# Input projections of a hybrid encoder layer: from f32r pairs to stored, scaled f16 pairs

## The chip, the cores and the metric

The kernel runs on one core of one Trainium2 chip. The metric is the device time of one execution in microseconds (us), taken as the median of several runs. The engines are TensorE (PE in the profile; its weight loads are PEld), VectorE (DVE), ScalarE (ACT), GpSimd (POOL) and SyncE (SP), which here issues all DMAs; SPq is its queue.

## What is computed

One layer of a streaming encoder for 2048 tokens of width 1024. The parts that matter here:

```python
h = rms_norm(x, norm1_g)                  # x * rsqrt(mean(x^2) + eps) * g, by row
p = h @ w_in                              # 1024 x 2560, one combined projection
q, k, v = p[:, :512], p[:, 512:1024], p[:, 1024:1536]
gb, gc, hin, u = four groups of 256 columns
q, k = rms_norm per head of 64            # then banded attention, own chunk + 8 before
y_conv = gb * dwconv3_causal(gc * hin)
y_pool = trailing means of u, minus u, mapped by pool_w, scaled
x = x + concat(y_attn, y_conv, y_pool) @ w_out
x = x + square(relu(rms_norm(x) @ w1)) @ w2
```

## The kernel before

Tokens are worked off in four blocks of 512 (`block(b)`, line 333); activations of x stand transposed, 8 tiles of 128 channels by 512 tokens. A product that needs more than one 16-bit pass is written as three matmuls (`mm3`, line 158): high*high, high*low, low*high. In the projections, the high and low halves are f32r tiles: `load_w` (line 136) loads 128x512 weights, copies them to f32r (ACT, or POOL for `w_cp`, line 140) and subtracts (DVE, line 141), anew in every block. `load_x` (line 338) multiplies x by the gain and splits it in the same way, with no division by the row's norm; that factor (rstd) goes later into q and k (through eps), into v, and into conv and pool through the broadcast row `R`.

Each block has two stages. **Projections**: `project(0)`, `project(1)`, `project(2)` for q, k and v, 96 matmuls of 128x512 each (tiles `a`); meanwhile q and k are normalised per head (`normalize`, line 373) and the first heads prepared (`prep`, line 391: transposes `tk` and `tq`, a trip of k through DRAM, copies into `qs`, `qx`, `kx`). **Attention and side work**: `weave` (line 74) fixes PE's order: two steps of `attention` for each head and tile of 128 queries (32 such units), and between them, at `RATE` steps of side work for each of attention's (`RATE0` in block 0), `side()`: the output projection of the block before (`o`, line 663), then the conv and pool projections (`cp`, `dense`, line 566) with what follows from them. `pace` (line 696) puts a step of the *survey* in at 2 of every 7 side steps: each loads two 256 KB tiles of w1 or w2 (`pr`, `ps`) and squares them on ACT, for the scales of the MLP. The survey's tiles, like those of x, take turns in a ring of three buffers, tag `x` of the pool `scr`.

A scheduler that simulates the program places everything that `weave` doesn't order: on ACT, DVE, POOL and in the DMA queue of SP it sets the order, and each engine works its list off in that order. After the four blocks comes the MLP (lines 721 to 955), whose matmuls are f16 (`b_u`, `b_d`) and which the change doesn't touch.

## Time and profile before

| | |
|---|---|
| runs | 2157.41, 2162.93, 2163.63 us, median 2162.93 |
| profiled execution | 2157.06 us, of which the span from first to last instruction is 2155.3 |
| PE busy | 2060.9 us, 96% of the span, 11136 matmuls |
| DVE busy | 1372.5 us, 64% |
| ACT busy | 1014.8 us, 47% |
| POOL busy | 700.5 us, 33% |
| mean granted TensorE clock | 0.983 of full speed |
| DMA | 378.19 MB, 55.3% of 16 engines' span |

Busy time is the union over an engine's instructions. Matmuls overlap in it: a single one is shown with some 0.4 us, yet the next starts after half of that, so their pace is read from starts. PEclk is the granted clock: 1.00 is 2.4 GHz, and half of it, 1.2 GHz, is the only other level; a mean between tells how much of a stretch ran at either.

### The profile page before, as it was taken

The numbers are of one execution on the slowest core, as the hardware profiler recorded it, in microseconds if no ns is written. First come the engines' busy times: TensorE is split into PE (matmuls) and PEld (weight loads), VectorE is DVE, ScalarE is ACT, GpSimd is POOL, SyncE is SP. The second block draws the span as 40 slices with busy tenths as digits, with TensorE's granted clock in tenths as the row PEclk, the third lists the DMA queues.
The fourth block names the chain that finished last, engine by engine and source line by source line (L and its number), as shares of the span: only waits on it lengthen the run. The fifth ranks groups of instructions, "written<-read, shape, count | busy, mean of one in ns | idle before, by whom it ended". The sixth has DMA issues, their size and how long they took to land.

```text
span 2155.3 us, 31723 instructions
## 1 busy us (share of the span) xinstructions
PE 2060.9 (96%) x11136; PEld 1269.3 (59%) x11136; DVE 1372.5 (64%) x2177; ACT 1014.8 (47%) x1939; POOL 700.5 (33%) x565
## 2 busy tenths in 40 slices
PE   8999999999899999989999889999999999999999
PEld 6777787878787878744444334444444444444444
DVE  7677566856577557897757897767743044253354
ACT  6465465646565655545647346446234151150330
POOL 4233054502211022365535555445522031030132
PEclk9999999999899999989999999999999999999999
DMA  8674587548754786654444684447843333333344
GB/s 298 179 216 154 171 261 218 169 142 251 224 172 140 223 236 183 212 176 158 168 157 147 239 279 142 167 156 269 276 121 102 103 103 100 101 97 108 103 143 155
DMA packets 207759, 378.19 MB, mean 175 GB/s; under 512 B 24688, under 2 KB 31984, under 8 KB 207600
## 3 DMA queue, kind: packets, MB, share of 16 engines
q1 hardware_dynamic: 207600, 376.18, 55.3%
q8 instruction: 87, 1.43, 0.3%
q14 instruction: 72, 0.59, 0.1%
HBM read 261.26 MB, written 98.04 MB: 167 GB/s over the span
## 4 chain that ended last, share of the span: by engine, by line
PE 71%; DVE 9%; DMA 7%; issue 5%; POOL 4%; ACT 3%; SPq 1%; POOLq 0%; DVEq 0%; ACTq 0%
PE b_d L787 20%; PE b_u L787 17%; PE a L159 4%; PE a L161 4%; PE a L160 4%; PE cp L159 2%; PE pt L497 2%; PE cp L160 2%; PE cp L161 2%; PE o L159 2%; PE o L161 2%; PE o L160 2%; PE y L512 2%; PE s L476 1%; PE s L477 1%
## 5 line engine op out<-in xcount | busy, mean ns | idle before, releaser
L787 PE MATMUL b_d<-ft_u,s_d 128*128 128x512 f16 x1152 | 264.6, 379 | 6.0 <-DVE ft_u L738 3.6
L787 PEld LDWEIGHTS <-s_u 128*128 128x128 f16 x1536 | 150.4, 98 | 197.2 <-issue 16.5
L787 PEld LDWEIGHTS <-s_d 128*128 128x128 f16 x1536 | 150.2, 98 | 190.6 <-issue 9.9
L908 DVE TENSOR_TENSOR acc<-acc,b_d 128x512 f32<-128x512 f32 x176 | 119.2, 682 | 184.4 <-PE b_d L787 181.3
L787 PEld LDWEIGHTS <-a_d 128*128 128x128 f16 x1152 | 113.3, 98 | 147.1 <-issue 13.0
L787 PEld LDWEIGHTS <-a_u 128*128 128x128 f16 x1152 | 112.6, 98 | 144.1 <-issue 9.5
L771 POOL TENSOR_TENSOR t1u<-u2u,c11u 128x512 f32<-128x512 f32 x32 | 42.5, 1329 | 439.2 <-ACT u2u L894 427.0
L787 PE MATMUL b_d<-fb_u,a_d 128*128 128x512 f16 x768 | 183.4, 379 | 0.0
L159 PE MATMUL a<-wq,xg 128*128 128x512 f32 x384 | 152.4, 402 | 8.2 <-ACT wq L140 8.0
L161 PE MATMUL a<-wq,xg 128*128 128x512 f32 x384 | 154.2, 402 | 2.1 <-DVE xg L344 2.1
L160 PE MATMUL a<-wq,xg 128*128 128x512 f32 x384 | 153.3, 399 | 0.0
L486 ACT ACTIVATE sb<-sb,nm 128x640 f32<-128x640 f32 (+4 forms) x128 | 97.7, 763 | 108.8 <-DVE nm L480 107.2
L499 DVE SCALAR_TENSOR_TENSOR pp<-pt,pp 128x384 f16<-128x384 f32 (+1 forms) x224 | 102.5, 483 | 66.8 <-ACT pp L498 65.8
L787 PE MATMUL b_u<-xt,s_u 128*128 128x512 f16 x576 | 132.5, 384 | 11.4 <-ACT xt L737 6.0
L208 POOL TENSOR_TENSOR acc<-acc,sq 128x512 f32<-128x512 f32 x56 | 83.0, 1482 | 184.8 <-ACT sq L207 143.4
L787 PE MATMUL b_u<-zt,s_u 128*128 128x512 f16 x576 | 126.9, 379 | 0.0
L480 DVE CUSTOM_DVE_ANT_0 sb<-s,b 128x640 f32<-128x640 f32 (+4 forms) x128 | 93.9, 734 | 36.3 <-PE s L477 34.9
L159 PE MATMUL o<-mix,wo 128*128 128x512 f32 x256 | 108.6, 425 | 2.7 <-DVE xo L678 2.7
L140 POOL CAST wc<-rwc 128x512 fp32r<-128x512 f32 x64 | 41.2, 643 | 211.1 <-PE cp L161 92.2
L159 PE MATMUL cp<-xg,wc 128*128 128x512 f32 x256 | 109.5, 428 | 0.0
L141 DVE TENSOR_TENSOR wq<-rwq,wq 128x512 fp32r<-128x512 f32 x96 | 77.5, 815 | 48.8 <-ACT wq L140 48.7
L285 POOL TENSOR_TENSOR pq<-pq,pq 128x512 bf16<-128x512 bf16 x32 | 38.3, 1196 | 208.4 <-ACT pq L282 207.7
(267 smaller groups left out, 4696.1 us busy)
## 6 DMA issues: line engine op xcount, KB each, us to landing
rwq<-w_qkv SPq DMA_DIRECT2D x96, 256.0 KB, 2.9
pr<-w SPq DMA_DIRECT2D x64, 256.0 KB, 4.0
rwc<-w_cp SPq DMA_DIRECT2D x64, 256.0 KB, 4.1
rwo<-w_out SPq DMA_DIRECT2D x64, 256.0 KB, 3.7
ps<-w SPq DMA_DIRECT2D x64, 256.0 KB, 4.0
r_u<-w SPq DMA_DIRECT2D x64, 256.0 KB, 2.9
wd<-s_u SPq DMA_DIRECT2D x64, 256.0 KB, 2.4
r_d<-w SPq DMA_DIRECT2D x64, 256.0 KB, 2.9
```

What stands on the lines that cost most here:

```text
L141: (lo or ve).tensor_tensor(out=w[:, 1], in0=raw, in1=w[:, 0].bitcast(F32), op=ALU.subtract)
L159: te.matmul(out, ah, bh, start=start, stop=False)
L160: te.matmul(out, ah, bl, start=False, stop=False)
L161: te.matmul(out, al, bh, start=False, stop=stop)
L208: gp.tensor_tensor(out=acc, in0=acc, in1=q, op=ALU.add)
L480: ve.tensor_tensor_reduce(out=sb[:, :nk].rearrange("p (e k) -> p e k", e=ne), in0=s[:, :ne, :hk], in1=bi[:, 640 - nk :].rearrange("p (e k) ...
L486: exps.append(sc.activation(sb[:, :nk], sb[:, :nk], AF.Exp, bias=nmx, scale=-1.0, accum_out=st["l"][:, i, j : j + 1]))
L497: te.transpose(pt[:, m * P : (m + 1) * P], sb[:, c0 + m * P : c0 + (m + 1) * P], ident)
L499: ve.scalar_tensor_tensor(out=pp[:, 1, c0:c1], in0=pt[:, :n], scalar=PSC, in1=pp[:, 0, c0:c1], op0=ALU.mult, op1=ALU.subtract)
L512: te.matmul(st["y"][:, i, j], pp[:, pi, ms_], vv[:, vi], start=(m == 0 and r == 0), stop=(m == nkt - 1 and r == 2))
L787: te.matmul(bank, w[:, a, q * P : (q + 1) * P], xs[q][:, c], start=start and q == 0 and i == 0, stop=q == n - 1 and i == 2, skip_group_che ...
L908: ve.tensor_tensor(out=a, in0=a, in1=bk, op=ALU.add)
```

## The change

Every input projection gets f16 halves. `weight_scale` finds a power of two for each of four weight groups (q, k, v, conv+pool) from the largest absolute weight: `look` takes a maximum of each 128x512 tile on DVE, a transposing matmul (`mx`) and a reduction bring them together. In block 0 `make_pair` scales and splits the weights (ACT and DVE), two tiles to a pair, and writes each pair to DRAM (`wq16`, `wc16`); the later blocks load pairs of 512 KB with `load_pair`, without ACT, DVE or POOL. `next_x` now normalises rows before the split: it sums squares, makes rstd, broadcasts it into `rn`, and then scales each tile by gain and `rn` on DVE, copies it to f16 on ACT and subtracts on DVE. For blocks 1 to 3 it runs as part of the side work of the block before, with x loaded twice (`xs`, `x`) through the `x` ring; for block 0 it runs at the start, from tiles that stay. `R` and the factors by it go. The survey leaves block 0 and takes every third side step in blocks 1 to 3. `RATE0` is 0.5.

```diff
-RATE, RATE0 = 0.95, 0.45
+RATE, RATE0 = 0.95, 0.5
...
+    def load_pair(src, name, shape):
+        w = wsp.tile([P, 2, 2, 512], F16, tag="w", name=name)
+        sy.dma_start(w.rearrange("p k s n -> p (k s n)"), src.rearrange("p k n -> p (k n)"))
...
+    def make_pair(raws, dst, scale, name, shape):
+        w = wsp.tile([P, 2, 2, 512], F16, tag="w", name=name)
+        for k in range(2):
+            raw = raws[k]()
+            sc.activation(w[:, k, 0], raw, AF.Copy, scale=scale)
+            ve.scalar_tensor_tensor(out=w[:, k, 1], in0=raw, scalar=scale, in1=w[:, k, 0], op0=ALU.mult, op1=ALU.subtract)
+        sy.dma_start(dst.rearrange("p k n -> p (k n)"), w.rearrange("p k s n -> p (k s n)"))
...
+    def largest(m, nm):
+        t = pd("mx" + nm)
+        te.matmul(t[:, :P], m.broadcast_to([P, P]), ident, start=True, stop=True)
+        ve.tensor_reduce(out=m, in_=t[:, :P], axis=AX.X, op=ALU.max)
...
+    def look(raw, i):
+        ve.tensor_reduce(out=wm[:, i : i + 1], in_=raw, axis=AX.X, op=ALU.max, apply_absolute_value=True)
+
+    def weight_scale(c):
+        m = const.tile([P, 1], F32, name=f"mw{c}")
+        ve.tensor_reduce(out=m, in_=wm[:, 8 * c : 8 * c + (8 if c < 3 else 16)], axis=AX.X, op=ALU.max)
+        r, inv = largest(m, str(c))
+        ve.tensor_scalar(wscale[:, c : c + 1], inv, 8192.0, None, op0=ALU.mult)
...
+    def look_at_cp(i):
+        raw = scr.tile([P, 512], F32, tag="x", bufs=3, name=f"sc{i}")
+        sy.dma_start(raw, w_cp[i // 2, i % 2])
+        look(raw, 24 + i)
...
+        acc = po.tile([P, TB], F32, tag="acc2", name=f"accn{b}")
+        for k in range(KT):
+            sumsq(acc, part(k, "xs"), k == 0, scr)
+            yield
+        ms = token_cols(acc, f"ms1_{b}")
+        yield
+        r = rsqrt(sm, ms, NT, "r1")
+        rb = row_bcast(r, f"rb{b}")
+        rn = p1.tile([P, TB], F32, tag="rn", bufs=1, name=f"rn{b}")
+        sc.copy(rn, rb)
+        yield
+        for k in range(KT):
+            xr = part(k, "x")
+            ve.scalar_tensor_tensor(out=xr, in0=xr, scalar=g1s[:, k : k + 1], in1=rn, op0=ALU.mult, op1=ALU.mult)
+            sc.copy(xgs[k][:, 0], xr)
+            ve.tensor_tensor(out=xgs[k][:, 1], in0=xr, in1=xgs[k][:, 0], op=ALU.subtract)
+            yield
...
             for k in range(KT):
-                if c == 0:
-                    load_x(k)
-                w = load_w(w_qkv[c, k], f"wq{b}_{c}_{k}", 1)
...
+                if k % 2 == 0:
+                    if b:
+                        pair = load_pair(wq16[c, k // 2], f"wq{b}_{c}_{k}", 1)
+                    else:
+                        raws = [lambda j=j: first_raws[c % 2][:, j] for j in (k, k + 1)]
+                        pair = make_pair(raws, wq16[c, k // 2], wscale[:, c : c + 1], f"wq{b}_{c}_{k}", 1)
+                if b == 0:
+                    if c < 2:
+                        fetch(c + 1, k)
+                    if c:
+                        look_at_cp(8 * c - 8 + k)
...
-                    ve.tensor_tensor(out=hs, in0=t, in1=R, op=ALU.mult)
+                    sc.activation(hs, t, AF.Copy, scale=sback)
...
-                if 2 * n % 7 < 2:
+                if b and n % 3 == 0:
                     next(surveyed, None)
...
+            ahead = next_x(b + 1, nxgs) if nxgs else iter(())
+            for _ in c:
+                next(ahead, None)
+                yield
```

Where the instructions stand, at three places.

DVE at the start of block 0, before: x and weights are split tile by tile, from the 14th instruction on (`bi` and `nb` belong to the attention's bias tables).

```order
L184 TENSOR_TENSOR pw<-pwr,pw 128x256
L344 SCALAR_TENSOR_TENSOR xg_0_123<-x_0_136,col,xg_0_123 128x512
L141 TENSOR_TENSOR wq_0_0_143<-rwq_0_0_141,wq_0_0_143 128x512
L344 SCALAR_TENSOR_TENSOR xg_1_124<-x_1_158,col,xg_1_124 128x512
L141 TENSOR_TENSOR wq_0_1_167<-rwq_0_1_165,wq_0_1_167 128x512
```

The same with the change: this stretch stands behind 16 looks at the weights of q and k (`first`); `r1r` is the last step of rstd, `sc` a look at a tile of w_cp.

```order
L285 TENSOR_SCALAR wscale<-big_208 128x1
L289 RECIPROCAL epsc<-back 128x1
L279 TENSOR_REDUCE wm<-sc_501 128x1
L188 TENSOR_TENSOR r1r<-r1r,r1t 128x4
L290 TENSOR_TENSOR epsc<-epsc 128x1
L279 TENSOR_REDUCE wm<-sc_521 128x1
L156 SCALAR_TENSOR_TENSOR wq_0_0_270<-first,wscale,wq_0_0_270 128x512
```

So rstd's end and the first weight pair now come after all these looks; the 8 scalings of x follow after the 8 subtractions for q's weights.

DVE in block 0 between the projections of k and of v, before: four weight tiles of v (`wq_2`) are split ahead of k's normalisation (`ssk`, later `nk`).

```order
L141 TENSOR_TENSOR wq_2_0_637<-rwq_2_0_635,wq_2_0_637 128x512
L141 TENSOR_TENSOR wq_2_1_685<-rwq_2_1_683,wq_2_1_685 128x512
L141 TENSOR_TENSOR wq_2_2_702<-rwq_2_2_700,wq_2_2_702 128x512
L141 TENSOR_TENSOR wq_2_3_719<-rwq_2_3_717,wq_2_3_719 128x512
L378 TENSOR_REDUCE ssk_652<-sqk_0_653 128x8
```

With the change, where `a_1` are the sums of k's projection and `mx_661` is the matmul that gathers v's largest weight; on PE it stands behind the last matmul of k's projection.

```order
L491 TENSOR_TENSOR nk_786<-a_1_2_490,rqr 128x512
L491 TENSOR_TENSOR nk_786<-a_1_3_491,rqr 128x512
L266 TENSOR_REDUCE mw_659<-mx_661 128x1
L267 TENSOR_SCALAR mw_659<-mw_659 128x1
L246 TENSOR_SCALAR big_665<-mw_659 128x1
L247 TENSOR_TENSOR pow_666<-big_665,mw_659 128x1
L248 TENSOR_TENSOR pow_666<-pow_666,big_665 128x1
L249 TENSOR_TENSOR pow_666<-pow_666,mw_659 128x1
L250 RECIPROCAL big_665<-pow_666 128x1
L286 TENSOR_SCALAR back<-pow_666,gm 128x1
L309 TENSOR_REDUCE vm<-vn 128x1
L285 TENSOR_SCALAR wscale<-big_665 128x1
```

v's scale, and with it every weight pair of v, now comes after all of k's normalisation.

ACT in block 1, in the second half of attention, before: exponentials (`sb`), copies of transposed scores (`pp`) and the survey (`pq`).

```order
L486 ACTIVATE sb_5_0_4218,l_2_3911<-sb_5_0_4218,nm_5_0_4219 128x640
L282 ACTIVATE pq_0_4249<-pr_0_4247 128x512
L282 ACTIVATE pq_1_4253<-pr_1_4251 128x512
L498 ACTIVATE pp_4_3_4258<-pt_4_3_0_4259 128x384
L498 ACTIVATE pp_4_3_4258<-pt_4_3_384_4265 128x256
L486 ACTIVATE sb_5_1_4312,l_2_3911<-sb_5_1_4312,nm_5_1_4313 128x640
```

The same two exponentials with the change, where `xs` are tiles of the next block's x.

```order
L591 ACTIVATE sb_5_0_4142,l_2_3861<-sb_5_0_4142,nm_5_0_4143 128x640
L341 ACTIVATE pq_0_4173<-pr_0_4171 128x512
L341 ACTIVATE pq_1_4177<-pr_1_4175 128x512
L746 ACTIVATE uh<-cp_7_4008,back 128x512
L223 ACTIVATE sq<-xs_1_4247 128x512
L603 ACTIVATE pp_4_3_4182<-pt_4_3_0_4183 128x384
L603 ACTIVATE pp_4_3_4182<-pt_4_3_384_4189 128x256
L223 ACTIVATE sq<-xs_2_4285 128x512
```

Between two exponentials stand two more squares of freshly loaded tiles and a copy of conv and pool's sums.

## Rows read from the trace of the kernel before

**Rows 1.** Windows by stage: length, busy time (count) by engine, PEclk, DMA share, GB/s.
```profile
8.00:82.00 74.00, 74.00 (x317) 59.54 (x318) 58.55 (x120) 38.83 (x67) 24.84 (x22) 1.00 0.78 252
82.00:172.00 90.00, 81.51 (x587) 67.99 (x586) 69.23 (x167) 54.96 (x135) 33.99 (x40) 0.94 0.71 210
172.00:243.00 71.00, 69.85 (x329) 56.00 (x328) 46.87 (x83) 33.13 (x58) 14.58 (x12) 1.00 0.46 144
252.00:410.00 158.00, 153.05 (x1217) 131.84 (x1217) 109.81 (x223) 97.03 (x210) 70.15 (x82) 0.97 0.71 221
...
486.00:646.00 160.00, 154.56 (x1204) 133.11 (x1203) 110.24 (x224) 98.38 (x237) 34.46 (x38) 0.96 0.72 215
...
721.00:882.00 161.00, 153.31 (x1211) 132.19 (x1210) 106.93 (x222) 98.20 (x241) 27.61 (x29) 0.97 0.67 198
```

**Rows 2.** Waits of PE up to 1000 us: total us, times, longest.
```profile
PE a L161 <- DVE xg L344: 2.1, 3, 1.2
```

**Rows 3.** Timeline of PE, block 0's projections: two starts, 45 matmuls apart.
```profile
48.02 0.40 PE L160 MATMUL a<-wq,xg 128*128 128x512 f32 x1
...
58.56 0.40 PE L160 MATMUL a<-wq,xg 128*128 128x512 f32 x1
```

**Rows 4.** Chain that ended last, in the MLP: start, us, what.
```profile
1571.22 72.52 PE b_u L787 x336
```

**Rows 5.** Timeline of PE, first matmuls of the program: start, duration.
```profile
10.69 0.63 PE L160 MATMUL a<-wq,xg 128*128 128x512 f32 x1
11.11 0.63 PE L161 MATMUL a<-wq,xg 128*128 128x512 f32 x1
```

**Rows 6.** Windows, second 20 us: the columns of rows 1.
```profile
20.00:40.00 20.00, 20.00 (x91) 16.29 (x90) 17.56 (x42) 14.79 (x25) 9.45 (x8) 1.00 0.99 338
```

**Rows 7.** Tile x up to 45 us: ns min/median/max, first and last start.
```profile
L340 SPq DMA_DIRECT2D x<-xT x8: 327/328/432, 2.1 to 18.0; - x8
L343 ACT ACTIVATE xg<-x,col x8: 717/724/728, 6.0 to 23.2; 128x512 fp32r<-128x512 f32 x8
L344 DVE SCALAR_TENSOR_TENSOR xg<-x,col,xg x8: 736/1130/1801, 6.7 to 24.6; 128x512 fp32r<-128x512 f32 x8
...
DMA to landing us min/median/max: 3.8/4.9/5.2
```

**Rows 8.** Groups of DVE, 42 to 82 us: busy us, mean ns, idle before.
```profile
L141 DVE TENSOR_TENSOR wq<-rwq,wq 128x512 fp32r<-128x512 f32 x11 | 7.4, 687 | 4.3 <-ACT wq L140 4.3
...
L378 DVE TENSOR_REDUCE ssk<-sqk 128x8 f32<-128x512 f32 x4 | 2.7, 683 | 0.0
```

**Rows 9.** Timeline of ACT, k's normalisation in block 0.
```profile
54.30 2.71 ACT L377 ACTIVATE sqk<-a 128x512 f32<-128x512 f32 x4
```

**Rows 10.** Timeline of DVE, from k's normalisation to v's scale in block 0.
```profile
57.83 0.69 DVE L141 TENSOR_TENSOR wq<-rwq,wq 128x512 fp32r<-128x512 f32 x1
...
59.88 0.69 DVE L141 TENSOR_TENSOR wq<-rwq,wq 128x512 fp32r<-128x512 f32 x1 [0.34 <-ACT wq L140]
...
61.15 2.48 DVE L383 TENSOR_TENSOR nk<-a,rqr 128x512 f32<-128x512 f32 x4
...
67.58 0.69 DVE L250 TENSOR_REDUCE vm<-vn 128x1 f32<-128x512 f32 x1 [1.38 <-PE vn L248]
...
69.78 0.15 DVE L254 TENSOR_SCALAR vsc<-big 128x1 f32<-128x1 f32 x1
```

**Rows 11.** Timeline of PE, end of block 1's projections.
```profile
241.01 0.60 PE L396 MATMUL tq<-ident,nq 128*128 128x128 f32 x4
...
245.42 1.05 PE L221 MATMUL rb<-ident,r1r 128*128 128x128 f32 x8
...
251.34 0.38 PE L476 MATMUL s<-kx,qs 128*128 128x320 f32 x1 [3.48 <-DMA qs<-qlo]
```

**Rows 12.** Chain in block 1's attention.
```profile
323.36 6.30 DMA kx<-kd
329.73 5.17 DMA pr<-w
```

More of the change, by code (lines that the diff above doesn't have):

```diff
@@ L224, in trunk @@
     vsc = const.tile([P, 2], F32, name="vsc")
[L225 removed]
+    vacc = p1.tile([P, 512], F32, tag="rn", bufs=1, name="vacc")
     def power_above(p):
@@ L365, in project, with fetch @@
             return ac
+        if b == 0:
+            kept = [p1.tile([P, NT, TB], F32, tag="n" + nm, name=f"x0{nm}") for nm in "qk"]
+            raw2 = po.tile([P, 2, KT, TB], F32R, tag="mix", name="first")
+            first_raws = [raw2[:, i].bitcast(F32) for i in range(2)]
+            def fetch(c, k):
+                raw = first_raws[c % 2][:, k]
+                sy.dma_start(raw, w_qkv[c, k])
+                look(raw, 8 * c + k)
+                if c == 2:
+                    value_norms(k, raw)
+                if k == KT - 1:
+                    weight_scale(c)
+            gain_scale()
+            steps = next_x(0, xgs, kept)
+            for k in range(KT):
+                next(steps)
+            for k in range(KT):
+                fetch(0, k)
+            for _ in steps:
+                pass
         acq = project(0)
-        ms1 = token_cols(acc, f"ms1_{b}")
-        rstd = rsqrt(sm, ms1, NT, "r1")
-        epsq = sm.tile([P, NT], F32, tag="epsq", name=f"epsq{b}")
-        ve.tensor_scalar(epsq, ms1, EPS, None, op0=ALU.mult)
         def normalize(ac, nm):
@@ L448, in block @@
         acv = project(2, lambda k: next(steps) if k in EARLY else None)
[L449 to L451 removed]
+        if b == 0:
+            weight_scale(3)
         for i in range(NT):
             src = acv[i].rearrange("p (h d) -> p h d", h=H)
[L454 to L455 removed]
+            sc.activation(v[:, :, i, 0], src, AF.Copy, scale=vback)
+            ve.scalar_tensor_tensor(out=v[:, :, i, 1], in0=src, scalar=vback, in1=v[:, :, i, 0], op0=ALU.mult, op1=ALU.subtract)
         if b < NB - 1:
@@ L458, in block @@
                 sy.dma_start(vd[b % 2, h], v[:, h].rearrange("p t s d -> p (t s d)"))
-        rb = row_bcast(rstd, f"rb{b}")
-        sc.copy(R, rb)
         mix = po.tile([P, 2, KT, TB], F32R, tag="mix", name=f"mix{b}")
@@ L567, in dense @@
             t = pd(f"cp{b}_{g}")
+            pair = weights.next()
             for half in range(2):
-                w = weights.next()
+                w = pair[:, half]
                 for kk in range(4):
@@ L643, in convpool @@
                     ve.tensor_copy(uh[:, j, 0:16], uh[:, j, TB : TB + 16])
-                ve.tensor_tensor(out=uh[:, j, 16:], in0=t, in1=R, op=ALU.mult)
+                sc.activation(uh[:, j, 16:], t, AF.Copy, scale=sback)
                 yield
@@ L702, in block, with raw_cp @@
         cp_order = (6, 7, 0, 1, 2, 3, 4, 5)
-        cp_loads = [lambda g=g, half=half: load_w(w_cp[g, half], f"wc{b}_{g}_{half}", 4, **CPW(gp, ve, g, half)) for g in cp_order for half in range(2)]
+        if b:
+            cp_loads = [lambda g=g: load_pair(wc16[g], f"wc{b}_{g}", 4) for g in cp_order]
+        else:
+            def raw_cp(g, half):
+                raw = wraw.tile([P, 512], F32, tag="raw", name=f"rwc{g}_{half}")
+                sy.dma_start(raw, w_cp[g, half])
+                return raw
+            cp_loads = [lambda g=g: make_pair([lambda h=h: raw_cp(g, h) for h in range(2)], wc16[g], wscale[:, 3:4], f"wc{b}_{g}", 4) for g in cp_order]
         prev_loads, prev_outproj, prev_stats = prev_out
@@ L712, in side @@
                 yield
-            yield from c
+            ahead = next_x(b + 1, nxgs) if nxgs else iter(())
+            for _ in c:
+                next(ahead, None)
+                yield
+            for _ in ahead:
+                yield
         weave(tc, attention(first), pace(side()), RATE if b else RATE0)
-        return out_loads, outproj, stats
-    prev_out = ([], lambda w: (), lambda: ())
+        return (out_loads, outproj, stats), nxgs
+    prev_out, xgs = ([], lambda w: (), lambda: ()), x_pairs(0)
     for b in range(NB):
-        prev_out = block(b, prev_out)
+        prev_out, xgs = block(b, prev_out, xgs)
     scales()
```

78 lines of the change are left out of this document (49 added, 29 removed).

## The prediction

> **What bounds the kernel now.** I read the stages first [rows 1]. Up to 882 us TensorE is busy nearly throughout: in the projections it is idle for 0 us of 74 in block 0 and 1.2 of 71 in block 1. DVE is busy for 59 of 74 us at the start and ACT for at most 62% anywhere, so before 882 us the time is TensorE's stream plus its gaps. The gaps lie in attention: 8.5 us in block 0, then 5.0, 5.4 and 7.7 us, 18.1 in blocks 1 to 3. After a gap the clock is at its lower level for a while; one minus the mean clock, times the stretch, is what that costs: 5.4 us in block 0, and 4.7, 6.4 and 4.8, 15.9 us, in the others. All that can be won by removing gaps is therefore 34 us in blocks 1 to 3 and 14 us in block 0's attention.
>
> Then the pace of one matmul. 45 f32r matmuls of the projections took 58.56 - 48.02 = 10.54 us, 234.2 ns each [rows 3]; 336 f16 matmuls of the same size in the MLP took 72.52 us, 215.8 ns each [rows 4]. The difference is 18.4 ns. All other work of the change must hide behind this stream or lengthen it.
>
> **Faster matmuls.** 1920 matmuls change type: 3 x 96 for q, k, v and 192 for conv and pool, in each of four blocks. Block 0's q, k and v I cost with its start, below. For the rest: 192 in block 0's attention save 3.5 us, 864 in the later projections 15.9 us and 576 in the later attentions 10.6 us: 30.0 us in all.
>
> The Trainium skill ("TensorE: Matmul & The Clock Gate", section "Wait — 56ns, not 53.3ns?") gives the start-to-start time at the full clock as the columns over 2.4 GHz plus 2.5 ns, 215.7 ns for 512 columns, and ties it to no type. By that, the f16 rows agree and the f32r rows do not; by the page alone this term would be nothing and the sum 30 us higher.
>
> **Block 0's start.** Today the first matmul starts 8 us into the span and projections end at 82 [rows 1]. With the change, nothing runs before x's row norms and q's weight scale, and both need complete passes. I follow the lists of the section on the change, in us from the start of the span.
> - *Loads.* 24 tiles (x, weights of q, of k) are issued ahead. The first lands at 2.1 + 3.8 = 5.9 [rows 7]; at the 338 GB/s seen with the DMAs 99% busy [rows 6] each further one takes 0.78 us. x is there at 11.3, q's weights at 17.5, k's at 23.7.
> - *Scale and norm.* A look costs 0.68 us [rows 8] and keeps up with the loads. The last step of rstd stands behind all 16 looks, two bias steps and one look at w_cp: about 28.
> - *Splits.* Then DVE does 8 subtractions for q's weights at 0.74 (the short form of L344 [rows 7]) with two more looks, until 35, 8 scalings of x until 41, two looks and bias steps, and 8 subtractions for x from 44 to 50. Matmuls of the high halves can start at 37, but the stream only flows from 44.6.
> - *q.* 90 matmuls are left. Some ten run at the lower clock, at 0.42 us [rows 5]; the rest at 215.8 ns. End: 66.
> - *k.* Its scale stands behind 8 looks at v's weights and 10 at w_cp. The latter share three buffers, each with some 4.9 us from issue to landing [rows 7]. I get 63 for the scale and 65 for the first pair if all DVE work takes its short form. L344's median was 1.13 us, against 0.74 at least [rows 7], and POOL sums squares beside this; for 8 subtractions that is 3 us. I take 68, hence k's end at 68 + 96 x 0.2158 = 88.7.
> - *v.* Its scale now waits for k's end and stands behind k's normalisation. Before, that work went from 54.30 to 63.63 [rows 9, 10], with two subtractions of 0.69 between that now are gone, and the steps from a maximum to a scale took 67.58 to 69.93, 2.4 us [rows 10]. The squares start some 2 us before k's projection ends, so v's scale is there at 88.7 - 2 + 8.0 + 2.4 = 97, and the ACT copy of 0.72 [rows 7] gives the first weights at 98; with handovers I say 99. TensorE stands still for 10 us here, restarts at the lower clock (2 us) and ends at 99 + 20.7 + 2 = 122.
>
> So block 0's projections end at 122 and not 82: **40 us lost**. Bounds: if scalings and subtractions overlap the looks better and the second gap of 7.6 us vanishes, 32; if all 40 scalings and subtractions take 0.39 us more, and half of that shows, and the loads land slower, 50. I take 40, the value that the short forms and one correction give.
>
> The Trainium skill ("SBUF — State Buffer", "SBUF: two separate sides") says that a DVE instruction with two SBUF inputs and a GpSimd instruction that reads SBUF exclude each other for a whole instruction. By that the 3 us above are what seven POOL sums cost; if the rule did not bite, k would start at 66 and the loss be 38. L344's spread is in favour of it.
>
> **Block 0's attention.** DVE loses 15 weight subtractions and 8 multiplications by `R`, and gains 8 subtractions for w_cp and 16 instructions of `next_x`, about as much; ACT loses the survey's squares and gains copies. No change beyond the 3.5 us, with 14 us of gaps as the bound of a gain.
>
> **Blocks 1 to 3.** The weights' copies and subtractions go: 120 subtractions at 0.69 us at least [rows 8], over 80 us of DVE. DVE has slack there, so this alone gives nothing. PE's waits for split x at a block's start, 2.1 us, go [rows 2]. The first scores of a block waited 3.5 us for a DMA that follows the transposes `tq` [rows 11]; what covers that DMA shrinks, by the `rb` matmuls (0.8 us, moved away) and 18 matmuls at 18.4 ns: 1.1 us a block, **3.4 us lost**. The pair loads move as many bytes as the f32 loads did, at DMA shares of 0.46 [rows 1]: hidden; if that cover went, the projections would wait for 512 KB every 5.2 us.
>
> Attention's gaps are the open price. The chain there runs through a transfer of `kx` (6.30 us), then the survey's `pr` (5.17 us), for which ACT waits with the next copies of scores queued behind it [rows 12]. The change does not shorten these transfers. It puts 22 survey steps in each block instead of 19, and in blocks 1 and 2 sends 16 more tiles of x through the same three buffers, whose ACT instructions stand between the exponentials. Bounds: all gaps vanish, -34 us; or buffers limit: in the second half of attention 22 survey tiles and 16 of x, each holding a buffer for 4.9 us of landing and about 2 of use, take 38 x 6.9 / 3 = 87 us, in a half of some 75: 12 us too long in each of two blocks, +25. I take +4, near the middle, since what ends these waits is not touched and the traffic rises by little.
>
> **Sum:** 40 - 30.0 - 2.1 + 3.4 + 4 = +15.3 us. The profiled execution took 2157.06 us, so 2172.4 on its scale; the median of the runs shown is 5.9 us higher, and I forecast 2178.2 against it. About 0.3%, 6.5 us, is what can be told from no change here.
>
> **Rivals.**
> - *Gaps close* (0.22). If DVE's and POOL's load, not the DMAs, sets the gaps, half of the 48 us goes: 40 - 30.0 - 2.1 + 3.4 - 24 = -12.7, 2150. It decides if ACT's waits in attention end with DVE. For it: 80 us less DVE work, and scores waiting on DVE in block 0; against it: the chain through DMAs [rows 12].
> - *A cheaper start* (0.20). 32 us instead of 40, gaps as they are: 32 - 30.0 - 2.1 + 3.4 = +3.3, 2166, no change that can be told.
> - *The ring of three* (0.17). ACT waits for x tiles in blocks 1 and 2: +25 in place of +4, 2199. For it: the two families of tiles alternate in one ring. Against it: mean DMA shares of 0.71 and 0.72 leave room [rows 1].
> - *One pace for both types* (0.02). If f16 matmuls with these operands start 234 ns apart, as the f32r ones do, the 30.0 us fall away: +45.3, 2208. Only the MLP's f16 matmuls were seen at 216 ns [rows 4], with other operands; that the type sets the pace is likelier by far. The Trainium skill's rule above would lead to this rival.
>
> **How the numbers follow.** My own forecast has 0.39. Faster by over 0.3%: 0.22; within 0.3%: 0.20; slower: 0.39 + 0.17 + 0.02 = 0.58. The range goes from 2147 to 2202: it leaves out the lower half of the first rival, half of the third and the last, about 2 in 10. The forecast's own range, from its start's bounds, is 2170 to 2188.
>
> **What would show it.** Matmuls of `a` and `cp` start 216 ns apart. The first of them starts near 37 us, flow begins near 45, and block 0's projections end near 122, with TensorE idle for some 10 us just before v's. In blocks 1 and 2, ACT's waits for `x`, `xs`, `pr` and `ps` add up to about what they were. I am wrong about the start if v's projection begins before 90 us, and about the gaps if TensorE's idle time in attention of blocks 1 to 3 falls under 10 us or rises above 30.

## The result and the profile after

The changed kernel takes **2226.28 us**, median of four runs (2218.37 to 2234.78), beside 2160.17 us for the kernel before (2154.24 to 2163.63): ratio **1.0314, 95% interval 1.0277 to 1.035**. It is slower by 66 us, not by 15, and lies outside the range. The profiled execution is the slowest of the four, 2234.78 us with a span of 2232.9, so the stages below hold 8.5 us more than the median does.

| us | before | after | forecast of the difference |
|---|---|---|---|
| span's start to block 0's first scores | 82.8 | 126.9 (+44.1) | +40 |
| attention of blocks 0, 1, 2 | 88.8, 157.3, 159.0 | 98.3, 182.1, 173.3 (**+48.6**) | -10.5 by pace, +4 by gaps |
| attention of block 3 | 157.4 | 154.4 (-3.0) | -3.5 |
| projections of blocks 1, 2, 3 | 79.7, 76.5, 75.7 | 70.4, 69.7, 72.3 (-19.5) | -14.6 |
| last projection work and the MLP | 1278.1 | 1285.4 (+7.3) | 0 |

A stage runs from one first start on TensorE to the next: attention from a block's first scores to the next block's first `a` (in block 3 to the first matmul `mx` of the MLP's scales), projections from there to the next first scores. The MLP's code is the same; from its first matmul to the end of the span it took 1254 to 1266 us in the profiles of this study, so its few us are scatter.

Windows of after by these stages (columns of [rows 1]; attention of block 0, projections of 1, and so on in turn):

```profile
126.92:225.20 98.28, 84.56 (x603) 54.07 (x604) 67.34 (x170) 55.06 (x133) 7.58 (x6) 0.91 0.66 201
225.20:295.58 70.38, 66.06 (x331) 31.72 (x331) 24.79 (x53) 17.83 (x31) 2.25 (x3) 0.99 0.41 121
295.58:477.60 182.02, 159.74 (x1195) 120.49 (x1196) 102.26 (x211) 107.80 (x228) 72.37 (x77) 0.91 0.74 223
...
547.33:720.70 173.37, 151.95 (x1196) 115.58 (x1197) 99.91 (x212) 107.81 (x243) 46.95 (x47) 0.95 0.75 228
...
793.01:947.40 154.39, 147.43 (x1163) 113.75 (x1164) 88.28 (x192) 101.17 (x253) 15.62 (x13) 0.96 0.72 217
```

The same stretches of before:

```profile
82.84:171.60 88.76, 80.27 (x582) 67.27 (x582) 68.03 (x163) 53.95 (x133) 33.59 (x40) 0.94 0.70 210
251.34:408.60 157.26, 152.48 (x1213) 131.80 (x1214) 108.41 (x222) 95.63 (x207) 68.83 (x81) 0.97 0.72 221
485.10:644.10 159.00, 153.47 (x1197) 132.43 (x1197) 108.34 (x221) 96.48 (x233) 34.46 (x38) 0.96 0.72 216
719.80:877.20 157.40, 149.66 (x1163) 129.18 (x1164) 102.70 (x213) 96.05 (x237) 27.61 (x29) 0.97 0.69 203
```

Length minus PE busy is TensorE's idle time: 8.5 + 4.8 + 5.5 + 7.7 = 26.5 us before, 13.7 + 22.3 + 21.4 + 7.0 = 64.4 after, 38 us more. One minus PEclk, times the length, is what the lower clock took: by these rounded values 21 us before, 40 after, 19 us more (16 if only the time in which matmuls ran is counted). Block 3, whose attention carries no `next_x`, lost nothing, though the survey is as dense there as in blocks 1 and 2: 37 of its loads are issued in that attention, 31 before.

Timeline of PE in after, block 0's start (start, duration, what, idle before and its releaser):

```profile
33.76 0.61 PE L175 MATMUL a<-wq,xp 128*128 128x512 f16 x1 [5.62 <-ACT xp L423]
...
41.38 0.61 PE L177 MATMUL a<-wq,xp 128*128 128x512 f16 x1 [4.88 <-DVE xp L424]
...
65.10 0.38 PE L176 MATMUL a<-wq,xp 128*128 128x512 f16 x1 [1.18 <-DVE wq L156]
...
94.20 0.76 PE L265 MATMUL mx<-ident,mw 128*128 128x128 f32 x2 [6.75 <-DVE nk L491]
...
99.03 1.44 PE L175 MATMUL a<-wq,xp 128*128 128x512 f16 x3 [1.17 <-ACT wq L155]
...
122.45 0.38 PE L177 MATMUL a<-wq,xp 128*128 128x512 f16 x1
122.67 0.38 PE L175 MATMUL cp<-xp,wc 128*128 128x512 f16 x1
122.88 0.38 PE L176 MATMUL cp<-xp,wc 128*128 128x512 f16 x1
```

This is the start as forecast: first matmul at 33.8 (37), flow from 41.4 (44.6), k's first pair at 65.1 (65 to 68), k's end at 94.20 - 6.75 = 87.4 (88.7), v's start at 99.0 (99), the end at 122.7 (122). The last three starts are 216 ns apart.

The long stops in the middle of attention, in blocks 1 and 2, stand before `ms`, the matmuls of the next block's row norms:

```profile
437.20 1.84 PE L229 MATMUL ms<-ones,accn 128*128 128x1 f32 x8 [5.68 <-DVE mix L719]
...
442.69 1.92 PE L237 MATMUL rb<-ident,r1r 128*128 128x128 f32 x8
...
683.31 1.84 PE L229 MATMUL ms<-ones,accn 128*128 128x1 f32 x8 [8.42 <-DVE mix L719]
```

The releaser is no producer of `accn`: `mix` reads `pl`, the earlier tenant of the PSUM bank that `ms` is written to. The chain of waits in after, 396 to 450 us, shows what made `mix` late:

```profile
413.17 3.21 DMA xs<-xT
416.46 0.63 ACT sq L223
...
423.66 6.50 DMA xs<-xT
430.25 0.63 ACT sq L223
430.88 0.64 ACT pp L603 x2
431.52 0.42 issue
431.94 0.73 ACT yc L733
432.69 1.23 DVE yc L734
433.94 1.52 DVE yc L735
435.46 0.94 DVE z L729
436.40 0.67 DVE mix L719
437.20 1.84 PE ms L229 x8
```

ACT stands at `sq` until the transfer of an x tile lands; behind it in ACT's queue stand the copies of transposed scores (`pp`) and `yc`; DVE's steps on `yc` wait for that, and `mix` stands behind them in DVE's queue. ACT's waits for DMAs in block 1's attention (295.58 to 477.60 us; total, times, longest), and the one kind of the same stage before:

```profile
ACT pq L341 <- DMA pr<-w: 17.8, 8, 7.0
ACT sq L223 <- DMA xs<-xT: 8.0, 6, 2.0
...
ACT accn L220 <- DMA xs<-xT: 4.2, 1, 4.2
```

```profile
ACT pq L282 <- DMA pr<-w: 5.4, 4, 3.9
```

In blocks 1 and 2 together ACT waited 15.2 us for `pr`, `ps` and `xs` before and 54.8 after; the forecast's sign was that these waits stay about what they were. In block 0, where no survey runs, it is DVE that stands, at the second load of x (`x`), and the copies of scores behind it stop TensorE; DVE, then PE, in after:

```profile
181.15 0.75 DVE L422 SCALAR_TENSOR_TENSOR x<-x,g1s,rn 128x512 f32<-128x512 f32 x1 [6.55 <-DMA x<-xT]
```

```profile
182.16 0.24 PE L617 MATMUL y<-v,pp 128*128 128x64 f16 x1 [4.68 <-DVE pp L604]
```

### The profile page after: what moved, and what is told of

Its sections match the earlier page's. It is cut to its first block, busy times and chain, and to the rows that moved or that the text cites. A ratio compares the mean times of both kernels' runs of the same rounds, so it can differ in the third digit from the quotient of the medians.

```text
span 2232.9 us, 31343 instructions
## 1 busy us (share of the span) xinstructions
PE 2054.8 (92%) x11146; PEld 1108.4 (50%) x11146; DVE 1303.6 (58%) x2146; ACT 997.5 (45%) x1905; POOL 648.9 (29%) x501
## 4 chain that ended last, share of the span: by engine, by line
PE 58%; DMA 14%; DVE 14%; issue 5%; ACT 4%; POOL 4%; SPq 1%; POOLq 0%; DVEq 0%; ACTq 0%
PE b_d L905 20%; PE b_u L905 17%; DMA xs<-xT 3%; PE a L175 2%; PE a L176 2%; PE a L177 2%; PE pt L602 2%; DMA r_d<-w 2%; PE o L175 1%; PE cp L175 1%; DMA pr<-w 1%; PE cp L176 1%; PE cp L177 1%; PE o L176 1%; PE o L177 1%
## 5 line engine op out<-in xcount | busy, mean ns | idle before, releaser
L1026 DVE TENSOR_TENSOR acc<-acc,b_d 128x512 f32<-128x512 f32 x176 | 119.3, 682 | 185.5 <-PE b_d L905 182.2
L175 PE MATMUL a<-wq,xp 128*128 128x512 f16 x384 | 147.8, 387 | 7.5 <-ACT xp L423 5.6
L177 PE MATMUL a<-wq,xp 128*128 128x512 f16 x384 | 146.9, 384 | 4.9 <-DVE xp L424 4.9
L176 PE MATMUL a<-wq,xp 128*128 128x512 f16 x384 | 148.1, 386 | 1.2 <-DVE wq L156 1.2
L905 PE MATMUL b_u<-zt,s_u 128*128 128x512 f16 x576 | 126.9, 379 | 0.0
L175 PE MATMUL o<-mix,wo 128*128 128x512 f32 x256 | 111.3, 436 | 6.4 <-DVE xo L780 5.8
L602 PE MATMUL pt<-ident,sb 128*128 128x128 f32 x560 | 86.7, 278 | 27.8 <-DVE pp L604 24.1
L176 PE MATMUL o<-mix,wo 128*128 128x512 f32 x256 | 105.6, 413 | 0.0
L177 PE MATMUL o<-mix,wo 128*128 128x512 f32 x256 | 105.5, 412 | 0.0
L175 PE MATMUL cp<-xp,wc 128*128 128x512 f16 x256 | 101.9, 398 | 2.9 <-ACT r2s L794 2.9
```

What stands on the lines that cost most here:

```text
L175: te.matmul(out, ah, bh, start=start, stop=False)
L176: te.matmul(out, ah, bl, start=False, stop=False)
L177: te.matmul(out, al, bh, start=False, stop=stop)
L602: te.transpose(pt[:, m * P : (m + 1) * P], sb[:, c0 + m * P : c0 + (m + 1) * P], ident)
L905: te.matmul(bank, w[:, a, q * P : (q + 1) * P], xs[q][:, c], start=start and q == 0 and i == 0, stop=q == n - 1 and i == 2, skip_group_che ...
L1026: ve.tensor_tensor(out=a, in0=a, in1=bk, op=ALU.add)
```

## The experiments

Three theories for attention at first. **Ring**: the second load of x through three buffers stops ACT, and ACT stops TensorE. **Bank**: `ms` and `rb` wait for a PSUM bank that the pool branch holds. **Survey pace**: the survey's steps are too dense beside `next_x`. Two more came up on the way: **load** (ACT and DVE have too much to do beside the exponentials) and **order** (two small matmul groups stand in TensorE's fixed order and stop it whenever their input is late). Each table gives the time from the span's start to the end of block 0's attention, since work moves across the first scores, then attention of blocks 1, 2, 3.

### x loaded once, and the bank

`e1_one_load` loads x once, three tiles ahead, into the place where its pair will lie; squares and scaling read it there, and no raw tile of x goes through the ring (the scaled tile still takes a buffer of it). `e2_psum_t` only moves `ms` and `rb` to another bank; `e3_one_psum` does both; `e4_no_survey` is after without the survey.

```diff
-            xr = part(k, "x")
+            return xgs[k].rearrange("p s n -> p (s n)").bitcast(F32)
...
+            load(k + 3)
+            sumsq(acc, place(k), k == 0, scr)
```

```diff
-        ms = token_cols(acc, f"ms1_{b}")
+        ms = token_cols(acc, f"ms1_{b}", "t")
-        rb = row_bcast(r, f"rb{b}")
+        rb = row_bcast(r, f"rb{b}", "t")
```

> Edit: the next block's x is loaded once, straight into the memory of the f16 pair that it will become, three tiles ahead; the squares and the scaling both read it there. The second load of each tile goes, and no load of x passes through the ring of three any more. Attention (first scores to the first matmul of the next projection, or to the matmuls of the last scale in block 3) took 98.3, 182.0, 173.4 and 154.4 us in blocks 0 to 3 of the changed kernel, 88.8, 157.4, 159.0 and 157.3 before. Theory 'ring': ScalarE waits for x tiles behind three shared buffers and holds the copies of scores back. Then attention of blocks 1 and 2 falls by 12 us or more each, and the whole by 30 or more. Rival 'bank': the matmuls of the row norms wait in TensorE's order for one of two PSUM banks that a dense group holds; then no more than 10 us go. Rival 'survey pace': no more than 10 us go.

> Edit: only the PSUM tiles ms1 and rb of the next block's row norms move from the tag d (two banks, of which an open dense group holds one) to the tag t (three banks). Theory 'ring': only the waits of ms themselves can go, 5.7 us in block 1 and 8.4 in block 2, so at most 14 us and likely under 8. Rival 'bank': attention of blocks 1 and 2 falls by 12 us or more each, and the whole by 25 or more. Rival 'survey pace': under 8 us.

> Both edits: x loaded once into the pair's memory, and ms1 and rb in the tag t. If either theory, ring or bank, names the whole cause between them, attention of blocks 0 to 2 comes to what block 3 shows, the stage before the change less 3 us (some 86, 154 and 156 us), and the whole falls by 45 us or more, to 2180 or less. If the survey's pace is the cause, the fall is under 15 us.

> The survey (its loads, squares, sums and its norms' matmuls) is left out and its two results are set to one; everything else stays. Theory 'survey pace': 22 survey steps a block in blocks 1 to 3 are too many beside next_x; then attention of blocks 1 and 2 falls by 15 us or more each and that of block 0, which holds no survey, stays at 98. Theory 'ring': x tiles alone still wait for their loads, as in block 0, where attention is 9.5 us longer than before without any survey; blocks 1 and 2 fall by 8 to 15 us each. Rival 'bank': under 5 us each.

| kernel | to end of att. 0 | att. 1 | 2 | 3 | median | ratio |
|---|---|---|---|---|---|---|
| before | 171.6 | 157.3 | 159.0 | 157.4 | 2160.17 | |
| after | 225.2 | 182.1 | 173.3 | 154.4 | 2226.28 | 1.0314 [1.0277, 1.035] |
| e1 | 213.2 | 163.6 | 160.2 | 154.3 | 2184.62 | 1.0134 [1.0119, 1.0149] |
| e2 | 224.6 | 174.6 | 169.8 | 152.5 | 2218.62 | 1.0308 [1.0281, 1.0334] |
| e3 | 215.7 | 159.5 | 161.3 | 152.6 | 2189.58 | 1.0154 [1.0132, 1.0176] |
| e4 | 224.1 | 156.2 | 152.5 | 141.6 | 2168.11, one run | |

Each ratio is taken against runs of the kernel before made beside it (medians 2152.7 to 2156.2 us in the experiments), so the ratios compare, and the medians only nearly.

e1 does what the ring theory expected of it: attention of blocks 1 and 2 falls by 18.4 and 13.1 us, and 1.8 hundredths of the ratio go, some 39 of the 66 us. About 6 of these lie ahead of block 0's first scores (126.9 to 121.0), where x is loaded once in both kernels; they are not the ring's. Nor does e1 part the ring from what goes with it: it halves the transfers of x and issues them earlier, too, and no run gives `after` itself a longer ring. Windows of e1, its four attentions:

```profile
121.00:213.20 92.20, 81.97 (x604) 53.09 (x605) 67.35 (x170) 55.83 (x134) 7.58 (x6) 0.94 0.73 218
282.40:446.00 163.60, 150.71 (x1195) 114.64 (x1196) 102.37 (x212) 107.10 (x227) 73.30 (x79) 0.97 0.74 222
516.70:676.90 160.20, 150.59 (x1195) 115.16 (x1196) 99.17 (x216) 108.56 (x248) 46.84 (x47) 0.96 0.74 227
748.40:902.70 154.30, 145.60 (x1163) 112.16 (x1164) 88.70 (x192) 101.04 (x253) 15.58 (x13) 0.96 0.72 217
```

Idle time falls from 64.4 to 41.4 us and the lower clock's cost from 40 to 23, together 40, at the same busy times of ACT (107.1 against 107.8 us in block 1) and nearly the same bytes per second. The stop of 4.68 us in block 0 is gone.

The bank alone is worth nothing that can be told: 0.0006 of the ratio. e3 missed what was expected if ring and bank were the whole cause: 86, 154 and 156 us in blocks 0 to 2, and 2180 us or less. In e3 `ms` no longer waits, but `rb` behind it does, for the steps of rstd; timeline of PE in e3, block 1 then block 2:

```profile
405.24 0.95 PE L229 MATMUL ms<-ones,accn 128*128 128x1 f32 x8
...
411.69 1.28 PE L237 MATMUL rb<-ident,r1r 128*128 128x128 f32 x8 [3.50 <-DVE r1r L188]
...
644.20 1.65 PE L237 MATMUL rb<-ident,r1r 128*128 128x128 f32 x8 [3.20 <-DVE r1r L188]
```

The wait has moved by one step. The survey costs time inside attention too: without it blocks 1 to 3 shrink by 26, 21 and 13 us, and the 13 are in a block with no `next_x` at all. By its expectation (15 us or more in blocks 1 and 2, nothing in block 0) e4 speaks for the survey's pace; but leaving the survey out also empties the ring, so it does not part the two. That block 3 lost nothing with 37 survey loads in place of 31 speaks against the pace alone.

### What of next_x stops TensorE

All on e1. `e11_no_next_x` leaves the whole of it out in blocks 1 to 3 (they use block 0's pairs), `e13_no_norm_mm` only `ms`, rstd and `rb`, `e14_no_squares` only the sums of squares, `e15_no_scale` only scaling and split.

```diff
-        ms = token_cols(acc, f"ms1_{b}")
...
+        else:
+            yield
+            rn = p1.tile([P, TB], F32, tag="rn", bufs=1, name=f"rn{b}")
+            ve.memset(rn, 1.0)
```

> On e1. The preparation of the next block's x (loads, squares, norms, scaling, splits) is left out for blocks 1 to 3: each of them projects block 0's x again, from the same tiles. All else stays, so attention holds no next_x in any block. In e1 attention took 92.2, 163.6, 160.2 and 154.3 us. Theory 'what is left of the loss in attention is next_x itself, its ScalarE and VectorE work and the matmuls of its norms in TensorE's order': blocks 0 to 2 come to 85 to 87, 153 to 157 and 153 to 157 us, the stage before the change less the 3 us of faster matmuls. Rival 'the survey, which is denser in blocks 1 to 3 now': block 0 gains, blocks 1 and 2 stay over 159.

> On e1, blocks 1 to 3: the matmuls ms and rb of the next block's norms and the steps from a sum to rstd are left out, the spread rstd is set to one. Loads, squares, scaling and splits stay. In e1 attention of blocks 0 to 2 took 92.2, 163.6 and 160.2 us, without any next_x 87.1, 156.6 and 151.5. Theory 'TensorE's order': what is left costs time because ms and rb stand in TensorE's fixed order and wait for a chain of ScalarE, POOL and VectorE; then this run comes to within 2 us of the values without next_x. Rival 'load': ScalarE's and VectorE's added work delays scores and their copies; then this run stays within 2 us of e1.

> On e1, blocks 1 to 3: the squares of the next x and their sums are left out (8 instructions of ScalarE and 7 of POOL a block), the sum is set to one; ms, rb, loads, scaling and splits stay. Theory 'TensorE's order': the chain before ms is gone but the one before rb stays, so part of the loss goes, some 1 to 4 us in each of blocks 0 to 2. Rival 'load': ScalarE loses 5 us of work a block in that stretch, and 1 to 4 us go as well; the two differ in e13 and e15.

> On e1, blocks 1 to 3: the scaling and the splits of the next x are left out (16 instructions of VectorE and 8 of ScalarE a block); each block projects block 0's x again. Loads, squares, ms and rb stay. Theory 'TensorE's order': attention of blocks 0 to 2 stays within 2 us of e1. Rival 'load': it comes to within 3 us of the values without next_x, as these are two thirds of the added work.

| kernel | att. 0 | 1 | 2 | 3 | one run, us |
|---|---|---|---|---|---|
| e1 | 92.2 | 163.6 | 160.2 | 154.3 | |
| e11 | 87.1 | 156.6 | 151.5 | 155.2 | 2166.03 |
| e13 | 87.2 | 157.5 | 154.0 | 153.1 | 2169.37 |
| e14 | 90.5 | 163.2 | 159.2 | 153.7 | 2182.51 |
| e15 | 89.6 | 164.4 | 161.4 | 154.5 | 2190.10 |

All of `next_x` costs e1 20.8 us in blocks 0 to 2. The 16 small matmuls and rstd account for 17.3 of them; eight squares and sums, or eight scalings, copies and subtractions, for 3.1 and 0.6. Block 3, where none of these edits acts, differs by 2.1 us between the five profiles, so the small numbers are scatter, and the 17.3 are not. It is the order, then, and not the load; each of e11 and e13 to e15 is one run. Windows of e13, blocks 0 to 2:

```profile
119.30:206.50 87.20, 78.08 (x588) 49.66 (x589) 58.77 (x153) 50.77 (x127) 7.71 (x6) 0.96 0.81 247
275.80:433.30 157.50, 148.07 (x1179) 113.12 (x1180) 100.64 (x207) 104.57 (x225) 73.78 (x79) 0.97 0.77 232
505.00:659.00 154.00, 146.69 (x1179) 112.36 (x1180) 97.88 (x209) 104.91 (x244) 46.74 (x47) 0.97 0.77 235
```

Against e1, 6.9 us are idle time, 4.0 the lower clock, and the remaining 6.4 fit the groups themselves, 1.0 us and more for each of the two in each of three blocks. Before the change these groups stood in the projections and took 1.6 us a block there, 4.9 in blocks 1 to 3, so that the move itself costs e1 some 12 us. In e1's timeline of PE, blocks 1 and 2, the waits stand there:

```profile
410.87 1.02 PE L229 MATMUL ms<-ones,accn 128*128 128x1 f32 x8 [3.00 <-DVE mix L722]
...
642.98 1.02 PE L229 MATMUL ms<-ones,accn 128*128 128x1 f32 x8 [2.91 <-DVE mix L722]
```

### More raw buffers

`e6_ring5` is e1 with five raw buffers (and one fewer for weight pairs).

```diff
-            raw = scr.tile([P, 512], F32, tag="x", bufs=3, name=f"ps{i}")
+            raw = scr.tile([P, 512], F32, tag="x", bufs=5, name=f"ps{i}")
```

> On e1. The ring of raw tiles, which now serves the survey and the scaled x, has five buffers instead of three; the ring of weight pairs has four instead of five, which pays for the space. In e1 ScalarE waited 31.4 us for pr and 18.5 us for ps in attention. Theory 'ring': with more tiles in flight these waits halve, and attention of blocks 1 to 3 (163.6, 160.2, 154.3 in e1) falls by 4 us or more each, the whole by 12 or more. Rival: the loads are late for another reason (the order of issue on SyncE, or traffic); then under 5 us in all. A risk: four pairs are too few ahead and the projections of blocks 1 to 3 slow.

2174.55 us, 1.0087 [1.0056, 1.0117]: some 10 us under e1, where 12 or more were expected. Attention of blocks 1 to 3 is 160.1, 152.8 and 153.8 us, 3.5, 7.4 and 0.5 less. ACT's waits for `pr` and `ps` there fall from 44.7 us in e1 to 2.6. So three buffers still hold up the survey with x's raw tiles gone from them, at the same traffic; but of 42 us of ACT's waits, TensorE felt some 11.

### The start

`e5_fixed_scale` is e1 with constant weight scales: no looks, no second reading of w_cp, no matmuls `mx`. `e7_start` keeps the search and puts DVE's queue of block 0 in another order by explicit dependencies (subtractions ahead of bias steps and looks, sums of squares on DVE, v's scale before k's normalisation). `e8_start_ring5` is e7 with five raw buffers; `e9_start6` moves the bias tables to POOL and w_cp's looks behind k's normalisation, and sets `rb` two side steps later; `e10_start6_ring5` is e9 with five buffers, paid for by two tiles that share a place with others.

```diff
     def weight_scale(c):
...
+        ve.memset(wscale[:, c : c + 1], 8192.0)
```

```diff
+                after(cut, ("scale", 0))
+                if splits:
+                    follow(tc, cut.ins, splits[-1].ins.name)
```

```diff
-        follow(tc, marks["look", 24 + i].ins, splits[-1].ins.name)
+        follow(tc, marks["look", 24 + i].ins, marks["nk"].ins.name)
```

> On e1 (x loaded once). The search for the four weight scales is left out: no look at a weight, no maximum, w_cp is not read for it, each scale is a constant. The norms of x, of v and all splits stay. In e1 the first matmul came at 33.6 us, the first scores at 121.0. Theory 'two complete passes set the start': then the first matmul still waits for x's norms and comes no earlier than 24 us, the projections run on without the 10 us before v's, and the first scores come at 92 to 105. If the search alone made the start late, they come at 83 to 88, as before the change; if it is hidden, after 115.

> On e1, block 0's start in another order, with the same work: VectorE adds x's squares (POOL did), the steps to rstd stand ahead of the looks, splits of x and of q's weights alternate, looks at k's weights stand behind q's splits, at v's behind k's, at w_cp behind v's, the bias tables' memsets go to POOL, v's scale is made in free PSUM banks in the middle of k's projection, and the squares for v's norms and for the next x stand behind k's copies and behind exponentials. Theory 'order of VectorE and the banks sets the start': first matmul at 25 to 30, no idle time before v's projection, first scores at 97 to 104 (121.0 in e1), the whole 17 to 24 us under e1. Rival 'the work itself is too much for VectorE': less than 10 us are won.

> e6 and e7 together. If both theories hold and add up, 30 us or more under e1, at 2155 or less, so at the kernel before or under it.

> e7 with three repairs that its trace asks for: the bias tables are made on POOL alone (in e7 VectorE stood still from 43.9 to 49.2 us behind one of them, with k's scale queued behind it), looks at w_cp stand behind k's norms (in e7 k's norms ended at 96.7 us, 19 us after k's projection, and the first scores waited for them), and the matmuls that spread rstd stand two steps later (in e7 TensorE waited 3.1 us for them in block 0's attention). Theory 'order of VectorE and the banks sets the start': k's projection follows q's without a gap, v's follows k's, first scores at 95 to 103 (113.4 in e7), block 0's attention at 90 to 95, the whole at 2155 to 2168. Rival 'the work itself is too much': first scores after 108.

> e9 with five buffers in the ring of raw tiles, paid for by placing the spread rstd in a tile of the output projection, so that the ring of weight pairs keeps its five. In e6 the longer ring took 10 us off, mostly in attention of blocks 1 and 2; in e8, with four weight pairs, block 0's attention lost 6 us to a wait for a pair of w_cp. Expected under e9 by 6 to 12 us; at 2145 to 2160.

| kernel | first `a` | first scores | end of att. 0 | median | ratio |
|---|---|---|---|---|---|
| e1 | 33.6 | 121.0 | 213.2 | 2184.62 | 1.0134 [1.0119, 1.0149] |
| e5 | 28.9 | 103.9 | 192.1 | 2163.16, one run | |
| e7 | 29.1 | 113.4 | 211.4 | 2181.40 | 1.0124 [1.0099, 1.0149] |
| e8 | 29.9 | 112.5 | 216.7 | 2177.90 | 1.0106 [1.0082, 1.0131] |
| e9 | 29.9 | 119.4 | 214.5 | 2184.80 | 1.0144 [1.0119, 1.0169] |
| e10 | 29.8 | 116.3 | 207.5 | 2165.98 | 1.0050 [1.0032, 1.0069] |

The search for the scales costs about 17 us up to the first scores. Another 6 of the 44 had gone in e1 (126.9 to 121.0), with k's projection, at 20.8 us instead of 24.0, and with a shorter wait before v's; why is open, and in the runs that share e1's start (e1, e11, e13 to e15) the first scores come at 119.3 to 124.1 us. The rest is that the first matmul starts at 28.9 us and not at 8.0; from there to the first scores e5 takes 75.0 us, the kernel before 74.8. x's norms stand ahead of that matmul in the code; no run left them out in block 0. Reordering won 7.6 us up to the first scores in e7 and had lost all but 1.8 of it by the end of block 0's attention. The expectations were 17 to 24 us under e1 for e7 and 30 or more for e8; 3 and 7 came. e10, expected 6 to 12 us under e9, came 19 under it, yet not under 2160. e9 is a plain miss: the looks at w_cp, moved out of one wait, made another, at the matmul that gathers w_cp's largest weight. Timeline of PE in e9:

```profile
113.93 0.79 PE L269 MATMUL mx<-ident,mw 128*128 128x128 f32 x2 [12.99 <-DVE mw L295]
```

### A version that loses no time

`e12_fixed_start` is e10 with constant scales, and x scaled and split tile by tile; `e16_early` moves one side step among v's projection, which should issue `qs` earlier; `e17_forced` pins the transposes `tk` and `tq` earlier on TensorE. The constant 8192 serves weights below 8 (8192 x 8 is f16's limit); these three, and e5, do not derive it from the data.

```diff
-EARLY = (0, 3, 5, 6)
+EARLY = (0, 3, 4, 5)
...
+                    if c == 2 and k in (5, 6):
+                        follow(tc, m.ins, marks["tk" if k == 5 else "tq"].ins.name)
```

> e10 (x loaded once, the start's order, five raw buffers) with the search for the weight scales left out as in e5: constant scales, which hold for weights up to 8 in size. VectorE scales and splits x tile by tile. Theory 'after the order is mended, what is left of the start is the search for scales, which stands before q, k and w_cp': first matmul at 22 to 25, TensorE busy from 27 on, first scores at 92 to 98 (116.3 in e10), the whole at 2138 to 2148, under the kernel before. Rival 'the norms and splits of x hold the start as well': first scores after 102, the whole above 2150.

> e12 with the transposes of q and the transfers of the first head pair's qs one step of v's projection earlier in every block (after k = 4 and 5 instead of 5 and 6). In e12 TensorE waited 7.5 us in block 0 and in the changed kernel 3.9 to 4.3 us in each later block for qs before the first scores. One step is 12 matmuls, 2.6 us. Expected: the first scores of block 0 some 3 us earlier, those waits shorter by 2 to 3 us in each later block, the whole 8 to 12 us under e12, at 2138 to 2148; if the transfers are late for traffic and not for the time of issue, no gain.

> e16's edit did not reach block 0: TensorE's order, which the scheduler makes, kept the transposes of q 12 matmuls ahead of the first scores, the transfers were issued at 92.1 us in e16 as in e12 (92.3), and the wait was 8.1 against 7.5 us. Here the order is forced: k's transposes stand ahead of v's matmuls of k = 5, q's ahead of those of k = 6, 24 matmuls ahead of the scores. If the time of issue decides, the transfers leave 3 us earlier, block 0's first scores come at 96 to 99 (101.2 in e16) and later blocks' waits for qs, 3.2 us at most in e16, stay under 3.5. If traffic decides (DMAs are 89 to 94% busy from 84 to 102 us), the first scores stay at 100 to 102. The whole: 2143 to 2152.

2152.75 us, ratio 0.9979 [0.9959, 0.9998]; 2151.98, 0.9982 [0.9968, 0.9995]; 2151.83, 0.9982 [0.9964, 1.0]. All three lie 0.2% under the kernel before, less than the 0.3% that can be told; e12 and e16 miss what was expected of them, 2138 to 2148 us. In e12 the first scores come at 100.6 us (92 to 98 expected), after a wait that the full stream had hidden:

```profile
92.69 0.38 PE L179 MATMUL cp<-xp,wc 128*128 128x512 f16 x1
100.57 0.45 PE L602 MATMUL s<-kx,qs 128*128 128x128 f32 x1 [7.51 <-DMA qs<-qhi]
```

e16 left it: in block 0 its transposes stand where e12's do, and the wait is 8.1 us. e17 removed it, though its first transfer of `qs` is issued at 92.6 us, as in e12 (92.3): the last one is issued at 95.9 us instead of 97.0 and nothing waits for it. The first scores come at 97.7 us, as its theory of the time of issue said (96 to 99), after a shorter wait for DVE:

```profile
97.67 0.30 PE L604 MATMUL s<-kx,qs 128*128 128x128 f32 x1 [2.95 <-DVE v L585]
```

The 2.9 us are gone by the end of block 0's attention, at 192.5 us in e17 and 192.4 in e12. What holds SP's queue before 92 us stays open.

## Why the prediction was wrong

- **Start: right.** +40 forecast, 122.7 against 82 at the projections' end measured, with every station within 3.5 us. The rival of a cheaper start falls. That the end fits to 1 us is partly luck. q's stream began 3 us early, and the 3 us that the forecast put on the splits of k's weights did not come there (none of the 24 splits of q's, k's and v's weights took over 0.75 us); k's projection then took 24.0 us in place of 20.7, with a wait of 1.2 us for its first split and seven starts 0.43 us apart behind it.
- **Pace: right.** Starts 216 ns apart in `a` and `cp`, as in [rows 4], not 234 as in [rows 3]. Block 3's attention gained 3.0 us where 3.5 were forecast, with more survey loads in it and a wait of 3.4 us for `tq` gone. The rival of one pace falls. The Trainium skill's rule that would lead to it ("TensorE: Matmul & The Clock Gate", section "Wait — 56ns, not 53.3ns?"), 215.7 ns for 512 columns, fits these f16 rows, 216 ns, and not the f32r rows, 234 ns.
- **The shorter cover of `qs`: right.** The first scores of blocks 1 to 3 waited 4.31, 1.98 and 3.85 us, 10.1 in all, against 7.6 before; 3.4 more were forecast, 2.5 came. The projections gained 5 us beyond the forecast: that is the time of `ms` and `rb`, 1.6 us a block before, which left them. `tq`'s waits for DVE, 9.9 us before and 1.2 after, lie in attention and were not in the forecast either; the other waits there grew by so much more.
- **The step that failed** is "Attention's gaps are the open price ... I take +4, near the middle, since what ends these waits is not touched and the traffic rises by little", with its bounds of -34 and +25. Measured: +38 us idle and +19 by the clock, +57, in the profiled executions. TensorE's idle time in attention of blocks 1 to 3 rose to 50.7 us, past the 30 that the forecast named as the sign of being wrong. Three things were wrong in it. First, the mechanism of its upper bound, x's tiles in the ring of three, did decide, and was given 0.17: e1, with x loaded once and past the ring, gets back some 33 of its 39 us behind the start. Mean DMA shares of 0.71 said nothing against it: after has 0.74 and 0.75 and stands still all the same, at the landing of single tiles. Second, that bound was too small: it counted blocks 1 and 2, but `next_x` runs in the attention of blocks 0 to 2 (block 0 alone got back 6.1 us in e1), and it counted idle time without the clock, which added 19 us to 38. Third, the matmuls `ms` and `rb` were moved from the projections into attention, and only the cover that `rb` gave to `qs` there was priced (0.8 us a block lost); their place in TensorE's fixed order, behind a chain through ACT, POOL and DVE, cost 17 us even in e1, by e13, or 12 beyond what they had cost in the projections.
- **Gaps close: wrong.** DVE was relieved as said (102 us busy for 108 in block 1's attention, 25 for some 47 in its projections [rows 1]), and the gaps grew: ACT's added waits end with DMAs.

What stays open: no run varies the lower clock alone, so its share in these accounts is read from the windows and not shown; how e1's gain divides between fewer transfers, their earlier issue and the buffers; how the survey's cost in blocks 1 and 2 divides between its faster pace and the buffers it shares; and the 8.5 us between the profiled execution and the median.

## What to carry to other kernels

When work is moved to a place "beside" other work, list its instructions on the in-order engines too: two groups of small matmuls, 2 us a block, cost nearly three times that where the tensor engine had to wait for them. A ring is to be costed by landing time and buffers, not by the mean share of the DMAs, and a tile that is needed twice is better loaded once into the place where its result will lie. An idle stretch of the tensor engine is to be priced with the lower clock behind it, here half as much again by the windows.
